# Scattering less from partitions 48-51 in seven groups, and issuing the first eight loads in halves

## The chip, the cores and the metric

The kernel runs on one core of one Trainium2 chip. The metric is the device time of one execution in microseconds (us). Each kernel was timed in several runs, beside runs of the kernel before on the same chip. A ratio is the mean time of one kernel's runs over the mean of the other's of the same rounds, which is not quite the ratio of the medians that I quote beside it. With every ratio comes a 95% interval.

## The reference

Each of 8 batches has 2048 rows of 2560 floats (10 KB a row) and 2048 scores. A row goes to the place that its score has in the sorted order of its batch.

```python
B, N, D = 8, 2048, 2560
order = np.argsort(scores, axis=1)
ranks = np.argsort(order, axis=1)
out[b_idx, ranks, :] = x
```

There are 168 MB to read and 168 MB to write. The arithmetic is counting, for each score, how many others are smaller.

## The kernel before

VectorE (DVE) counts the ranks, batch after batch. A batch's rows are moved in eight groups of 256 rows, two rows a partition. Most groups go through SBUF, the core's on-chip memory: GpSimd (POOL) issues a **load** of 2.5 MB into one of eight buffers, and later two indirect **scatters** of 128 rows each.

```python
GROUPS = [(256 * i, 2) for i in range(8)]
DIRECT = range(6)
...
BULK = [(b, g) for b in range(B) for g in range(len(GROUPS)) if g or b not in DIRECT]
NBUF = 8
LAG = 4
...
for k, (b, g) in enumerate(BULK):
    i = k % NBUF
    if k >= LAG and k + NBUF - LAG < len(BULK):
        scatters_done(pl, k - LAG)          # waits for all 16 increments of both scatters
        load(pl, k + NBUF - LAG, s_load[(k - LAG) % NBUF])
    ...                                     # wait for load k and for its ranks
    for j in range(GROUPS[g][1]):
        scatter(k, j)                       # 128 rows of 10 KB, indirect
```

The first group of batches 0 to 5 doesn't pass through SBUF. SyncE (SP) and ScalarE (ACT) each read 128 ranks a batch into registers and issue one DMA for each row, from HBM (the chip's main memory) to HBM, in loops of 16 rows. I call these **direct rows**: 768 on SP's queue and 768 on ACT's.

```python
for b in DIRECT:
    for h, (line, name) in enumerate(((sp, ENG.SP), (act, ENG.Activation))):
        ...
        with line.eng.Fori(0, half // G) as q:          # G = 16 rows a turn of the loop
            _, at = nc.values_load_multi_w_load_instructions(...)
            for i in range(G):
                ...
                line.eng.dma_start(
                    out=out_bytes[bass.ds(at[i], ROW)], in_=x_bytes[...],
                ).then_inc(s_rows[line], 16)
```

In the packet records of this kernel a direct row is cut into 16 pieces of 640 bytes (12288 such packets in each row queue, for 768 rows), one for each of the 16 DMA engines. A load or scatter over 128 partitions is 128 packets, of 20 KB (two rows; 7296 for 57 loads) or 10 KB (one row; 14848 for 116 scatters): eight an engine. The records of the engine that is left alone in the tail agree: eight scatter packets between one 4-byte semaphore packet of q0 and the next, and in each row queue a 640-byte packet and a 4-byte one by turns.

Of the kernel before, what the change touches and what calls it, by code (L numbers as in the profile page):

```python
# [7 lines left out]
P = 128  # L8
F32 = mybir.dt.float32
BF16 = mybir.dt.bfloat16  # L10
I32 = mybir.dt.int32
U8 = mybir.dt.uint8
OP = mybir.AluOpType
ENG = mybir.EngineType
# [26 lines left out]
def kernel(  # L41
# [6 lines left out]
    nc = tc.nc  # L48
    B, N, D = x.shape
    C = N // P  # L50
# [11 lines left out]
    LAG = 4  # L62
    G = 16

    STEPS = [(0, 1), (1, 2), (2, 4), (4, 8)]

    def first_col(g):
        return GROUPS[g][0] // P if g < len(GROUPS) else C
# [11 lines left out]
    acc = [pool.tile([P, B * C], F32, name=f"acc{i}") for i in range(3)]  # L80
    rank = pool.tile([P, B * C], F32, name="rank")
    rank_i = pool.tile([P, B * C], I32, name="rank_i")
    rows_i = {b: pool.tile([1, WIDE], I32, name=f"rows_i{b}") for b in DIRECT}
    xb = [pool.tile([P, MMAX * D], F32, name=f"x{i}") for i in range(NBUF)]
    ps_col = psum.tile([P, 512], F32, name="ps_col")
# [7 lines left out]
    with tc.tile_critical(no_gpsimd_drain=True):  # L93
# [12 lines left out]
        s_rows = {sp: nc.alloc_semaphore("rows_sp"), act: nc.alloc_semaphore("rows_act")}  # L106
        n_scat = [[0] * MMAX for _ in range(NBUF)]

        def load(line, k, sem):
            b, g = BULK[k]  # L110
            r, m = GROUPS[g]
            line.eng.dma_start(  # L112
                out=xb[k % NBUF][:, :m * D],
                in_=x[b, r:r + P * m, :].rearrange("(p j) d -> p (j d)", j=m),
            ).then_inc(sem, 16)


        sp.eng.dma_start(out=s_in[:], in_=scores).then_inc(s_scores, 16)
        load(sp, 0, s_first)


        t_zero = pl.did(nc.gpsimd.memset(ident[:], 0.0))  # L122
# [52 lines left out]
        def broadcast(b):  # L175
            pe.after(dve, t_copied)
            ticks = []
            for c in range(C):
                pe.did(
                    nc.tensor.transpose(  # L180
                        out=ps_all[:, P * c:P * (c + 1)],
                        in_=s_col[:, c, b:b + 1].to_broadcast([P, P]),
                        identity=ident[:],
                    )
                )
                if c % 4 == 3:
                    ticks.append(pe.n)
            return ticks
# [3 lines left out]
        dve.after(pl, t_mask)  # L192
        bc = broadcast(0)

        def ranks(b, g_lo, g_hi):

            for g in range(g_lo, g_hi):
                lo = first_col(g)
                m = GROUPS[g][1]
                for j in range(m):  # L200
                    col = b * C + lo + j
                    score = s_col[:, lo + j, b:b + 1]
                    dve.after(dve, dve.n)

                    def count(i, lo_c, hi_c, do, **how):
                        dve.did(
                            do(  # L207
                                out=trash[i][:, :P * (hi_c - lo_c)],
                                in0=s_all[:, P * lo_c:P * hi_c],
                                accum_out=acc[i][:, col:col + 1],  # L210
                                **how,
                            )
                        )

                    count(
                        0, lo, C, nc.vector.tensor_scalar,
                        scalar1=score, scalar2=None, op0=OP.is_lt, op1=OP.add,
                    )
                    if lo:
                        count(  # L220
                            1, 0, lo, nc.vector.tensor_scalar,
                            scalar1=score, scalar2=None, op0=OP.is_le, op1=OP.add,
                        )
                    count(
                        2, lo, lo + m, nc.vector.scalar_tensor_tensor,
                        scalar=score,
                        in1=mask[:, MMAX - j:MMAX - j + m, :].rearrange("p a b -> p (a b)"),
                        op0=OP.is_equal, op1=OP.mult,
                    )
            cols = slice(b * C + first_col(g_lo), b * C + first_col(g_hi))  # L230
            dve.after(dve, dve.n)
            dve.did(
                nc.vector.tensor_tensor(  # L233
                    out=rank[:, cols], in0=acc[0][:, cols], in1=acc[1][:, cols], op=OP.add
                )
            )
            dve.after(dve, dve.n)
            dve.did(
                nc.vector.tensor_tensor(  # L239
                    out=rank[:, cols], in0=rank[:, cols], in1=acc[2][:, cols], op=OP.add  # L240
                )
            )
            dve.after(dve, dve.n)
            tick = dve.did(
                nc.vector.tensor_copy(out=rank_i[:, cols], in_=rank[:, cols])  # L245
            )
            for g in range(g_lo, g_hi):
                t_bulk[b, g] = tick

        def rows_to_psum(b):  # L250
            pe.after(dve, dve.n)
            for j in range(GROUPS[0][1]):
                pe.did(
                    nc.tensor.transpose(  # L254
                        out=ps_row[:1, P * j:P * (j + 1)],
                        in_=rank[:, b * C + j:b * C + j + 1],
                        identity=ident[:],
                    )
                )

        def rows_to_bytes(b):
            dve.after(pe, pe.n)
# [11 lines left out]
        for b in range(B):  # L274
            dve.after(dve, dve.n)
            for q in range(4):
                dve.after(pe, bc[q])
                t_copied = dve.did(
                    nc.vector.tensor_copy(  # L279
                        out=s_all[:, 512 * q:512 * (q + 1)],  # L280
                        in_=ps_all[:, 512 * q:512 * (q + 1)],
                    )
                )
            steps = STEPS if b == 0 else [(0, len(GROUPS))]
            for lo, hi in steps:
                ranks(b, lo, hi)
                if lo == 0:
                    if b in DIRECT:
                        rows_to_psum(b)
                        rows_to_bytes(b)  # L290
                    if b + 1 < B:
                        bc = broadcast(b + 1)


        for b in DIRECT:
            for h, (line, name) in enumerate(((sp, ENG.SP), (act, ENG.Activation))):
                line.after(dve, t_rows[b])
                half = WIDE // 2
                with line.eng.Fori(0, half // G) as q:
                    _, at = nc.values_load_multi_w_load_instructions(  # L300
                        rows_i[b][:, bass.ds(half * h + q * G, G)],
                        engines=[name],
                        min_val=b * N * ROW,
                        max_val=(b * N + N - 1) * ROW,
                        skip_runtime_bounds_check_because=(
                            "a rank counts other scores of one batch of N, so it lies in 0..N-1"
                        ),
                    )
                    for i in range(G):
                        row = b * N + GROUPS[0][0] + half * h + i  # L310
                        line.eng.dma_start(
                            out=out_bytes[bass.ds(at[i], ROW)],
                            in_=x_bytes[bass.ds(q * (G * ROW) + row * ROW, ROW)],
                        ).then_inc(s_rows[line], 16)
        for line in (sp, act):
            line.wait(s_rows[line], 16 * len(DIRECT) * WIDE // 2)


        def scatters_done(line, k):
# [4 lines left out]
        def scatter(k, j):  # L324
            b, g = BULK[k]
            col = b * C + first_col(g) + j
            n_scat[k % NBUF][j] += 1
            nc.gpsimd.indirect_dma_start(  # L328
                out=out_flat,
                out_offset=bass.IndirectOffsetOnAxis(ap=rank_i[:, col:col + 1], axis=0),  # L330
                in_=xb[k % NBUF][:, j * D:(j + 1) * D],
                in_offset=None,
                element_offset=b * N * D,
            ).then_inc(s_scat[k % NBUF][j], 16)

        for k in range(1, NBUF):
            load(pl, k, s_load[k])
        for k, (b, g) in enumerate(BULK):
            i = k % NBUF
            if k >= LAG and k + NBUF - LAG < len(BULK):  # L340
                scatters_done(pl, k - LAG)
                load(pl, k + NBUF - LAG, s_load[(k - LAG) % NBUF])
            if k == 0:
                pl.wait(s_first, 16)
            else:
                pl.wait(s_load[i], 16 * (k // NBUF + (i > 0)))
            pl.after(dve, t_bulk[b, g])
            for j in range(GROUPS[g][1]):
                scatter(k, j)
# [34 lines left out]
```

## Time and profile before

| | before |
|---|---|
| time, median | 792.58 us (4 runs, 791.97 to 792.9) |
| span of the profiled run | 791.4 us |
| DVE, POOL busy | 50%, 18% |
| loads and scatters: packets of POOL's queue q0 | 24912 |
| SP's queue q1, ACT's queue q10 | 24736, 24576 |

The lines that say what bounds it, the DMA share by slices and the windows at the end, are in the prediction below. Here are the page's DMA queues (packets, MB, and the time of those packets as a share of the span of 16 engines):

```profile
q0 software_dynamic: 24912, 301.48, 89.5%
q1 hardware_dynamic: 24736, 10.60, 4.9%
q10 hardware_dynamic: 24576, 7.91, 4.0%
```

The engines spend nine tenths of the span on loads and scatters. And the two row queues, which with the first load move only 18.5 MB, need **as many packets** as these: 24576 = 768 rows x 16 engines x 2, as each piece of a row is followed by a 4-byte packet for its semaphore (on ACT's queue 12288 packets of 640 bytes and 12288 of 4).

### The profile page before, as it was taken

Reading aid. Unit: us, or ns where it says so; the run is one execution under the profiler, and the core shown is the slowest. Engines: PE = TensorE matmul, PEld = TensorE weight load, DVE = VectorE, ACT = ScalarE, POOL = GpSimd, SP = SyncE. Lnnn points to the kernel's source line nnn. Section 1 sums busy time; section 2 is a strip of 40 time slices with the busy share of each in tenths; the row PEclk is TensorE's granted clock in tenths of the full one; section 3 lists DMA queues with packets and bytes.
Section 4 is the critical chain, followed back from the end, with each engine's and each line's share of the span. In section 5 each row is a group of like instructions: output and inputs, shape, how many; then the busy total and the mean of one; then the engine's idle time right before and its main releaser. Section 6 shows DMA issues by size and latency. Waiting matters only on the chain.

```text
span 791.4 us, 7991 instructions
## 1 busy us (share of the span) xinstructions
PE 30.9 (4%) x156; PEld 27.6 (3%) x156; DVE 398.3 (50%) x809; ACT 0.0 (0%) x1; POOL 146.2 (18%) x182
## 2 busy tenths in 40 slices
PE   4000010020100200200000000000000000000000
PEld 3000010010100100200000000000000000000000
DVE  5999999999999999999992000000000000000000
ACT  0000000000000000000000000000000000000000
POOL 2114021212121211112121212121111212121000
PEclk9655555555555555655555555555555555555555
DMA  8999999999999999999999999999999999999960
GB/s 366 423 407 416 425 416 423 418 425 415 427 414 425 415 424 416 425 420 422 419 419 421 420 422 420 422 418 423 418 424 419 422 419 423 418 425 418 417 252 19
DMA packets 74239, 320.12 MB, mean 404 GB/s; under 512 B 27368, under 2 KB 51944, under 8 KB 51944
## 3 DMA queue, kind: packets, MB, share of 16 engines
q0 software_dynamic: 24912, 301.48, 89.5%
q1 hardware_dynamic: 24736, 10.60, 4.9%
q10 hardware_dynamic: 24576, 7.91, 4.0%
q14 instruction: 14, 0.11, 0.0%
q8 instruction: 1, 0.02, 0.0%
HBM read 167.84 MB, written 167.77 MB: 424 GB/s over the span
## 4 chain that ended last, share of the span: by engine, by line
DVE 43%; another core or an unknown queue 30%; POOL 8%; DMA 6%; issue 6%; PE 3%; POOLq 0%; SPq 0%
DVE trash L207 41%; POOL out_dram L328 6%; DMA x<-in_x_dram 6%; PE ps_all L180 2%; POOL x L112 2%; DVE s_all L279 1%; PE ps_row L254 0%; DMA s_in<-in_scores_dram 0%; PE ps_col L159 0%; DVE rank_i L245 0%; DVE rank L239 0%; DVE rank L233 0%; POOLq L350 0%; POOLq L28 0%
## 5 line engine op out<-in xcount | busy, mean ns | idle before, releaser
L207 DVE TENSOR_SCALAR_CACHE_REDUCE trash<-s_all,s_col 128x1792 bf16<-128x1792 f32 (+7 forms) x240 | 315.2, 1348 | 4.6
L328 POOL DMA_INDIRECT out_dram<-x,rank_i x116 | 112.3, 968 | 146.1 <-DVE rank_i L245 55.7
L112 POOL DMA_DIRECT2D x<-in_x_dram x57 | 32.1, 566 | 462.2 <-DMA out_dram<-x,rank_i 441.1
L207 DVE SCALAR_TENSOR_TENSOR trash<-s_all,s_col,mask 128x256 bf16<-128x256 f32 x128 | 61.6, 481 | 0.0
L180 PE MATMUL ps_all<-ident,s_col 128*128 128x128 f32 x128 | 26.5, 394 | 1.2 <-DVE s_all L279 0.8
L180 PEld LDWEIGHTS ps_all<-ident,s_col 128*128 128x128 f32 x128 | 25.1, 214 | 2.0 <-DVE s_all L279 1.1
L279 DVE COPY s_all<-ps_all 128x512 f32<-128x512 f32 x32 | 21.4, 689 | 6.0 <-PE ps_all L180 5.3
L207 DVE DVE_READ_ACCUMULATOR trash<-s_all,s_col 128x1 f32 x240 | 19.9, 83 | 0.0
L254 PE MATMUL ps_row<-ident,rank 128*1 128x128 f32 x12 | 3.5, 396 | 288.9 <-DVE rank_i L245 288.9
L207 DVE DVE_READ_ACCUMULATOR trash<-s_all,s_col,mask 128x1 f32 x128 | 10.7, 83 | 0.0
L254 PEld LDWEIGHTS ps_row<-ident,rank 128*1 128x1 f32 x12 | 0.5, 81 | 291.1 <-DVE rank_i L245 291.1
L264 DVE TENSOR_SCALAR rows_i<-ps_row 1x256 int32<-1x256 f32 x6 | 2.5, 411 | 4.1 <-PE ps_row L254 4.1
L167 DVE COPY s_col<-ps_col 128x128 f32<-128x128 f32 x1 | 0.3, 292 | 5.0 <-PE ps_col L159 5.0
L159 PE MATMUL ps_col<-ident,s_in 8*128 8x8 f32 x16 | 2.1, 264 | 4.1 <-DMA s_in<-in_scores_dram 4.1
L245 DVE CAST rank_i<-rank 128x16 int32<-128x16 f32 (+3 forms) x11 | 2.0, 180 | 0.4
L159 PEld LDWEIGHTS ps_col<-ident,s_in 8*128 8x128 f32 x16 | 2.0, 211 | 4.1 <-DMA s_in<-in_scores_dram 4.1
L239 DVE TENSOR_TENSOR rank<-rank,acc 128x16 f32<-128x16 f32 (+3 forms) x11 | 1.9, 170 | 0.4
L233 DVE TENSOR_TENSOR rank<-acc,acc 128x16 f32<-128x16 f32 (+3 forms) x11 | 1.9, 170 | 0.4
L140 POOL TENSOR_SCALAR_AFFINE_SELECT mask<-mask 128x256 f32<-128x256 f32 x2 | 0.8, 399 | 0.0
L152 DVE MEMSET acc<- 128x128 f32 x1 | 0.2, 165 | 1.1 <-SPq L93 1.1
L123 POOL MEMSET mask<- 128x512 f32 x1 | 0.5, 525 | 0.0
L122 POOL MEMSET ident<- 128x128 f32 x1 | 0.2, 204 | 0.5 <-SPq L93 0.5
(6 smaller groups left out, 0.7 us busy)
## 6 DMA issues: line engine op xcount, KB each, us to landing
x<-in_x_dram POOLq DMA_DIRECT2D x57, 2560.0 KB, 46.3
out_dram<-in_x_dram ACTq DMA_DIRECT2D x768, 10.0 KB
out_dram<-in_x_dram SPq DMA_DIRECT2D x768, 10.0 KB
x<-in_x_dram SPq DMA_DIRECT2D x1, 2560.0 KB, 13.2
out_dram<-x,rank_i POOLq DMA_INDIRECT x116, 51.2
s_in<-in_scores_dram SPq DMA_DIRECT2D x1, 64.0 KB
```

Of the source, the lines that this page charges most:

```text
L112: line.eng.dma_start(out=xb[k % NBUF][:, :m * D], in_=x[b, r:r + P * m, :].rearrange("(p j) d -> p (j d)", j=m),).then_inc(sem, 16)
L140: nc.gpsimd.affine_select(out=part, in_=part, pattern=[[0, MMAX], [-1, P]], compare_op=OP.is_ge, fill=0.0, base=-half, channel_multiplier=1,)
L159: nc.tensor.transpose(out=ps_col[:, B * c:B * (c + 1)], in_=s_in[:, r + j:r + m * P:m], identity=ident[:B, :B],)
L180: nc.tensor.transpose(out=ps_all[:, P * c:P * (c + 1)], in_=s_col[:, c, b:b + 1].to_broadcast([P, P]), identity=ident[:],)
L207: do(out=trash[i][:, :P * (hi_c - lo_c)], in0=s_all[:, P * lo_c:P * hi_c], accum_out=acc[i][:, col:col + 1], **how,)
L233: nc.vector.tensor_tensor(out=rank[:, cols], in0=acc[0][:, cols], in1=acc[1][:, cols], op=OP.add)
L239: nc.vector.tensor_tensor(out=rank[:, cols], in0=rank[:, cols], in1=acc[2][:, cols], op=OP.add)
L245: nc.vector.tensor_copy(out=rank_i[:, cols], in_=rank[:, cols])
L254: nc.tensor.transpose(out=ps_row[:1, P * j:P * (j + 1)], in_=rank[:, b * C + j:b * C + j + 1], identity=ident[:],)
L264: nc.vector.tensor_scalar(out=rows_i[b][:].rearrange("o (p j) -> o p j", p=P), in0=ps_row[:1, :WIDE].rearrange("o (j p) -> o p j", p=P), s ...
L279: nc.vector.tensor_copy(out=s_all[:, 512 * q:512 * (q + 1)], in_=ps_all[:, 512 * q:512 * (q + 1)],)
L328: nc.gpsimd.indirect_dma_start(out=out_flat, out_offset=bass.IndirectOffsetOnAxis(ap=rank_i[:, col:col + 1], axis=0), in_=xb[k % NBUF][:, ...
```

## The change

In seven groups (the fifth group of batches 1 to 7) the scatters leave out the rows of partitions 48-51: the ranks there get 2048 added, which a bounds check skips. These 4 partitions x 2 rows x 7 groups = 56 rows are issued as further direct rows: four groups (32 rows) by SP and three (24) by ACT. And the first eight loads are issued as two halves of one row (10 KB) a partition. I took the intent to be that the one slow DMA engine gets less to do. That these partitions are that engine's was my assumption.

```diff
+    THIN = [(b, 4) for b in range(1, B)]
+    HOLES = range(48, 48 + 4)
+    HALVED = range(8)
...
+            for j in range(m if k in HALVED else 1):
+                part = slice(j * D, (j + 1) * D) if k in HALVED else slice(0, m * D)
+                line.eng.dma_start(
+                    out=xb[k % NBUF][:, part], in_=rows[:, part]
+                ).then_inc(sem, 16)
...
+                if (b, g) in THIN:
...
+                            out=rank_i[:, cols], in0=rank[:, cols],
+                            scalar1=hole[:], scalar2=None, op0=OP.add,
...
+        def thin_rows(n, b, g):
+            line, name = ((sp, ENG.SP), (act, ENG.Activation))[n % 2]
...
+            for i in range(4 * m):
+                row = b * N + r + HOLES[i % 4] * m + i // 4
+                line.eng.dma_start(
+                    out=out_bytes[bass.ds(at[i], ROW)],
+                    in_=x_bytes[bass.ds(row * ROW, ROW)],
+                ).then_inc(s_rows[line], 16)
...
+                **(dict(bounds_check=N - 1, oob_is_err=False) if (b, g) in THIN else {}),
```

More of the change, by code (lines that the diff above doesn't have):

```diff
@@ L82 @@
     rank_i = pool.tile([P, B * C], I32, name="rank_i")
+    hole = pool.tile([P, 1], F32, name="hole")
+    thin_i = {k: pool.tile([1, 4 * MMAX], I32, name=f"thin_i{k[0]}_{k[1]}") for k in THIN}
     rows_i = {b: pool.tile([1, WIDE], I32, name=f"rows_i{b}") for b in DIRECT}
@@ L107 @@
         n_scat = [[0] * MMAX for _ in range(NBUF)]
+        n_load = [0] * NBUF
         def load(line, k, sem):
@@ L111, in load @@
             r, m = GROUPS[g]
-            line.eng.dma_start(
-                out=xb[k % NBUF][:, :m * D],
-                in_=x[b, r:r + P * m, :].rearrange("(p j) d -> p (j d)", j=m),
-            ).then_inc(sem, 16)
+            rows = x[b, r:r + P * m, :].rearrange("(p j) d -> p (j d)", j=m)
+            for j in range(m if k in HALVED else 1):
[3 more added lines that the diff above has]
+                ).then_inc(sem, 16)
+                if k:
+                    n_load[k % NBUF] += 1
         sp.eng.dma_start(out=s_in[:], in_=scores).then_inc(s_scores, 16)
         load(sp, 0, s_first)
+        loaded = {0: (s_first, 16 * (2 if 0 in HALVED else 1))}
         t_zero = pl.did(nc.gpsimd.memset(ident[:], 0.0))
@@ L193 @@
         bc = broadcast(0)
+        dve.did(
+            nc.vector.tensor_reduce(
+                out=hole[:],
+                in_=ident[:, HOLES[0]:HOLES[0] + 4],
+                axis=mybir.AxisListType.X,
+                op=OP.add,
+            )
+        )
+        dve.after(dve, dve.n)
+        dve.did(
+            nc.vector.tensor_scalar(
+                out=hole[:], in0=hole[:], scalar1=float(N), scalar2=None, op0=OP.mult
+            )
+        )
         def ranks(b, g_lo, g_hi):
@@ L248, in ranks, with rows_to_psum @@
                 t_bulk[b, g] = tick
-        def rows_to_psum(b):
+                if (b, g) in THIN:
+                    cols = slice(b * C + first_col(g), b * C + first_col(g + 1))
+                    dve.after(dve, dve.n)
+                    t_bulk[b, g] = dve.did(
+                        nc.vector.tensor_scalar(
+                            out=rank_i[:, cols],
+                            in0=rank[:, cols],
+                            scalar1=hole[:],
+                            scalar2=None,
+                            op0=OP.add,
+                        )
+                    )
+        def rows_to_psum(b, g):
             pe.after(dve, dve.n)
-            for j in range(GROUPS[0][1]):
+            for j in range(GROUPS[g][1]):
+                col = b * C + first_col(g) + j
                 pe.did(
@@ L255, in rows_to_psum @@
                         out=ps_row[:1, P * j:P * (j + 1)],
-                        in_=rank[:, b * C + j:b * C + j + 1],
+                        in_=rank[:, col:col + 1],
                         identity=ident[:],
@@ L259, in rows_to_psum, with thin_to_bytes @@
                 )
+        def thin_to_bytes(b, g):
+            m = GROUPS[g][1]
+            dve.after(pe, pe.n)
+            t_rows[b, g] = dve.did(
+                nc.vector.tensor_scalar(
+                    out=thin_i[b, g][:].rearrange("o (j i) -> o j i", j=m),
+                    in0=ps_row[:1, :P * m].rearrange("o (j p) -> o j p", j=m)[
+                        :, :, HOLES[0]:HOLES[0] + 4
+                    ],
+                    scalar1=float(b * N),
+                    scalar2=float(ROW),
+                    op0=OP.add,
+                    op1=OP.mult,
+                )
+            )
         def rows_to_bytes(b):
@@ L288 @@
                     if b in DIRECT:
-                        rows_to_psum(b)
+                        rows_to_psum(b, 0)
                         rows_to_bytes(b)
@@ L292 @@
                         bc = broadcast(b + 1)
+                for g in range(lo, hi):
+                    if (b, g) in THIN:
+                        rows_to_psum(b, g)
+                        thin_to_bytes(b, g)
+        n_rows = {sp: 0, act: 0}
+        def thin_rows(n, b, g):
+            line, name = ((sp, ENG.SP), (act, ENG.Activation))[n % 2]
+            r, m = GROUPS[g]
+            line.after(dve, t_rows[b, g])
+            _, at = nc.values_load_multi_w_load_instructions(
+                thin_i[b, g][:],
+                engines=[name],
+                min_val=b * N * ROW,
+                max_val=(b * N + N - 1) * ROW,
+                skip_runtime_bounds_check_because=(
+                    "a rank counts other scores of one batch of N, so it lies in 0..N-1"
+                ),
+            )
+            for i in range(4 * m):
[4 more added lines that the diff above has]
+                ).then_inc(s_rows[line], 16)
+                n_rows[line] += 1
+        todo = list(enumerate(THIN))
         for b in DIRECT:
+            while todo and todo[0][1][0] < b:
+                n, where = todo.pop(0)
+                thin_rows(n, *where)
             for h, (line, name) in enumerate(((sp, ENG.SP), (act, ENG.Activation))):
@@ L314 @@
                         ).then_inc(s_rows[line], 16)
+                n_rows[line] += half
+        for n, where in todo:
+            thin_rows(n, *where)
         for line in (sp, act):
-            line.wait(s_rows[line], 16 * len(DIRECT) * WIDE // 2)
+            line.wait(s_rows[line], 16 * n_rows[line])
         def scatters_done(line, k):
@@ L333, in scatter, with load_ahead @@
                 element_offset=b * N * D,
+                **(dict(bounds_check=N - 1, oob_is_err=False) if (b, g) in THIN else {}),
             ).then_inc(s_scat[k % NBUF][j], 16)
+        def load_ahead(k):
+            i = k % NBUF
+            load(pl, k, s_load[i])
+            loaded[k] = (s_load[i], 16 * n_load[i])
         for k in range(1, NBUF):
-            load(pl, k, s_load[k])
+            load_ahead(k)
         for k, (b, g) in enumerate(BULK):
-            i = k % NBUF
             if k >= LAG and k + NBUF - LAG < len(BULK):
                 scatters_done(pl, k - LAG)
-                load(pl, k + NBUF - LAG, s_load[(k - LAG) % NBUF])
-            if k == 0:
-                pl.wait(s_first, 16)
-            else:
-                pl.wait(s_load[i], 16 * (k // NBUF + (i > 0)))
+                load_ahead(k + NBUF - LAG)
+            pl.wait(*loaded[k])
             pl.after(dve, t_bulk[b, g])
```

## The prediction

Its sum: for the slow engine it is 786.75 - 21.3 + 1.9 + 0.35 = 767.7 us, for the second slowest 767.1 + 2.25 + about 0.4 = 769.7 us, so 17 us less and 775.5 us. The ground for the 21.3 us, that all 56 packets come off one engine, the slow one, and that the skipped indices leave nothing, was my assumption, and no trace had shown it.

> **What bounds the kernel now.** I read the page's shares and slices first, then the waits, then the tail in windows, then the times at which each DMA raised its semaphore. No compute engine is the bound: DVE is 50% busy, POOL 18%, and both are done long before the end. The DMA engines are full.
>
> ```profile
> PE 30.9 (4%) x156; PEld 27.6 (3%) x156; DVE 398.3 (50%) x809; ACT 0.0 (0%) x1; POOL 146.2 (18%) x182
> ...
> DVE  5999999999999999999992000000000000000000
> ...
> DMA  8999999999999999999999999999999999999960
> GB/s 366 423 407 416 425 416 423 418 425 415 427 414 425 415 424 416 425 420 422 419 419 421 420 422 420 422 418 423 418 424 419 422 419 423 418 425 418 417 252 19
> ```
>
> The third row is the one that counts: 420 GB/s in nearly every slice, until the last two. POOL's largest wait, 441 us for earlier scatters to free a buffer, is only this back-pressure. The windows over the end (stretch and length in us, busy time of five engines, clock, DMA share, GB/s) show what happens there:
>
> ```profile
> 740.00:755.00 15.00, 0.00 (x0) 0.00 (x0) 0.00 (x0) 0.00 (x0) 3.35 (x4) 0.50 1.03 416
> 755.00:765.00 10.00, 0.00 (x0) 0.00 (x0) 0.00 (x0) 0.00 (x0) 0.39 (x1) 0.50 0.89 348
> 765.00:770.00 5.00, 0.00 (x0) 0.00 (x0) 0.00 (x0) 0.00 (x0) 0.00 (x0) 0.50 0.09 35
> 770.00:786.50 16.50, 0.00 (x0) 0.00 (x0) 0.00 (x0) 0.00 (x0) 0.00 (x0) 0.50 0.06 26
> ```
>
> From 770 to 786.5 us the share is 0.06, which is one engine of 16 (0.0625), at 26 GB/s, about a sixteenth of the 416 of before. So **one DMA engine finishes some 20 us after the other fifteen**, and the kernel ends with it. It isn't one odd transfer. The last scatter's 16 semaphore increments come at 763.3 us (the first), +1.6 (the fourteenth), +4.1 (the fifteenth) and +23.8 (the last). That last increment was 2.8 us behind the first at 88 us, 6.4 at 192, 10.3 at 297, 13.8 at 402, 17.9 at 507, 20.8 at 612 and 23.4 at 716: one engine loses about 3.4 us in every 105 us. In the records of single packets, 10 KB scatter packets take 385 ns, but 575 of them take some 15 to 60 ns more, and these hardly ever overlap one another, as if they belonged to one engine.
>
> [...] Packet records carry no engine, so the trace can't confirm which one lags. [...] 16 increments spread over 23.8 us. [...] in the tail the lone engine alternates one scatter packet (10 KB), one packet of SP's row queue and one of ACT's.
>
> **The change part by part.** The costs are from the packet records of the tail, where one engine can be followed alone (start to next start): 381 ns for a 10 KB packet, 28 ns for the 640 B an engine moves of an HBM-to-HBM row, 6 ns for a semaphore packet. So one row costs every engine 28 + 6 = 34 ns. A 20 KB load packet takes 757 ns.
>
> Removed: seven groups x two scatters x four rows = 56 rows. [...] 56 x 381 ns = **21.3 us**. This nearly equals the lag of 23.8 us, and the groups are spread evenly (one a batch), so the lag should be knocked back by about 3 us in each batch from 1 on.
>
> Added on every engine: the same 56 rows HBM to HBM, 56 x 34 ns = **1.9 us**. The full engines can't hide it.
>
> Halving eight loads: 64 more packets an engine, each pair 2 x 381 - 757 = 5 ns dearer, 0.3 us, and eight semaphore packets, 0.05 us: **0.35 us**. What I think it is for: with one packet from each queue per turn, the rows are carried as fast as the loads and scatters have packets. From 20 us, when the rows begin, an engine has about 1541 load, scatter and semaphore packets and 1536 packets (768 rows, data and semaphore) in each row queue, an even match. The change lengthens SP's queue to 800 rows (1600 packets) and ACT's to 792; the halves that are still to come at 20 us give some 47 more turns. So row queues and scatters should still end together.
>
> Other added work: seven times on DVE a masked add and a small conversion with a wait on PE (about 0.2 + 0.4 + 0.7 us from like rows), 9 us over a DVE that idles half the span. Batch 1's ranks are there at 110.8 us and its first scatter lands at 143 us, so a microsecond or two is hidden. POOL's seven more load issues of 0.56 us come before its first scatter at 25.6 us. Hidden too.
>
> Sum, by when an engine ends (semaphore times):
> - the slow one: 786.75 - 21.3 + 1.9 + 0.35 = 767.7 us (766.3 if the 56 were slow packets at 25 ns more)
> - the second slowest (767.1 to 767.4, behind by 14 instruction-fetch packets of 0.31 us, I guess): 767.1 + 2.25 + about 0.4 for more code = 769.7 us
> - the other fourteen: 764.9 + 2.25 = 767.1 us.
>
> The end moves from 786.75 to about 769.7 us: 17 us less. Time 792.55 - 17 = **775.5 us**, a ratio of 0.978. Once the slow engine is level, the second slowest is the bound.
>
> **The rivals.**
> 1. **The holes are not on the slow engine**, or skipped indices lead to the remaining 124 rows being dealt out anew over 16 engines. Then the tail stays, each engine gets the 2.25 us (less up to 1.3 us if the saving is shared), and the time is 793 to 795 us. Against: 21.3 us fits the lag too well to be chance. For: nothing in the trace names the engine, and no scatter here has a bounds check.
> 2. **Row queues become the end.** The slow engine loses 56 turns, so at its last scatter it still has some 30 to 40 rows in each row queue. Run at 34 ns this is 2 to 3 us and is in the sum already; if rows without scatters run slower, or SP is held back by the full queue (its last row was issued at 759.6 us, with waits of 2.5 us and more for space), the end comes 2 to 5 us later: 777 to 780 us, and "same".
> 3. **More than hoped.** If the second slowest engine isn't touched by more code or the fetches fall on another engine, all end at 767 us and the time is 773 us.
> 4. **The tail was hidden anyway.** Against it: the span runs to 791.4 us with nothing but this engine at work after 770 us.
>
> **Range and chances.** I give the mechanism 85%; inside it the gain is 17 us give or take 2.5, and 2% is 15.9 us, so about two cases in three of these are over 2%. Predicted 775.5 us, range 770.5 to 782. Faster by over 2%: 0.57; within 2%: 0.41; slower: 0.02.
>
> **What would show each step.** In windows of the changed kernel the stretch with a DMA share of 0.06 is gone or under 4 us. The gap between the first and last of 16 increments swings between 2 and 7 us all along and doesn't grow to 24. GB/s in the middle slices stays at 420. The row queues have 1792 more packets in all for data (56 x 16) and as many semaphores. POOL still waits hundreds of us for scatters, and DVE ends near 410 us. I am wrong if the lone engine remains (rival 1), if row packets alone fill the last microseconds (rival 2), or if the halved loads run at a lower rate than 420 GB/s before 60 us.

## The result, and the profile after

The changed kernel takes **782.06 us** (4 runs, 781.49 to 782.53) against 792.58: 10.5 us less. The ratio is 0.9868, interval 0.9851 to 0.9885, so within 2%. I had said 775.5 us and a range up to 782.0. The sign and the cause of the gain were right, the gain is 0.62 of what I had worked out.

The changed kernel's slices (DMA share in tenths, GB/s) and its queues:

```profile
DMA  8999999999999999999999999999999999999995
GB/s 360 418 419 419 426 415 425 415 421 416 424 418 424 416 421 417 425 417 423 419 421 420 422 419 421 420 422 422 417 425 416 426 416 425 417 424 418 419 415 101
...
q0 software_dynamic: 25920, 300.90, 90.7%
q1 hardware_dynamic: 25904, 10.93, 5.5%
q10 hardware_dynamic: 25344, 8.16, 4.5%
```

The middle is as before at 420 GB/s. Before, the last two slices read 252 and 19 GB/s; now they read 415 and 101: the long tail is gone. But the windows over the end of the changed kernel (same columns as in the prediction) show another one:

```profile
755.00:760.00 5.00, 0.00 (x0) 0.00 (x0) 0.00 (x0) 0.00 (x0) 0.00 (x0) 0.50 1.02 412
760.00:765.00 5.00, 0.00 (x0) 0.00 (x0) 0.00 (x0) 0.00 (x0) 0.00 (x0) 0.50 1.04 321
765.00:770.00 5.00, 0.00 (x0) 0.00 (x0) 0.00 (x0) 0.00 (x0) 0.00 (x0) 0.50 0.99 86
770.00:775.00 5.00, 0.00 (x0) 0.00 (x0) 0.00 (x0) 0.00 (x0) 0.00 (x0) 0.50 0.18 9
```

From 765 to 770 us **all sixteen engines are busy (0.99) and move only 86 GB/s**. This is no lone engine, which would read 0.06. The share counts the time of packets, not their bytes, so these are packets that take long and carry little. The DMA view of the changed kernel from 763.5 us to the end names them:

```profile
q1 hardware_dynamic: 875, 0.28, 13.1%
q10 hardware_dynamic: 490, 0.15, 10.8%
q0 software_dynamic: 36, 0.29, 2.5%
```

875 + 490 packets of direct rows against 36 of scatters. In the same stretch of the kernel before there were 90 + 88. The records of single packets give the order of events: the last 10 KB scatter packet ends at 769.30 us (786.68 before), the last direct row at 773.29 us on ACT's queue and at **775.36 us on SP's**; the span ends 4.4 us later. So the scatters end near where I had expected (769.7 us), and 6.06 us of direct rows come after them. The question for the experiments is why the rows were late, and whether anything else hides in the difference.

### The profile page after: what moved, and what is told of

It is laid out like the page before. It is cut to its first block, busy times and chain, and to the rows that moved or that the text cites. A ratio compares the mean times of both kernels' runs of the same rounds, so it can differ in the third digit from the quotient of the medians.

```text
span 779.7 us, 8177 instructions
## 1 busy us (share of the span) xinstructions
PE 35.4 (5%) x170; PEld 30.5 (4%) x170; DVE 399.8 (51%) x825; ACT 0.0 (0%) x1; POOL 150.2 (19%) x189
## 4 chain that ended last, share of the span: by engine, by line
DMA 49%; another core or an unknown queue 19%; DVE 13%; POOL 7%; issue 6%; PE 1%; POOLq 0%; SPq 0%
DMA out_dram<-x,rank_i 43%; DVE trash L238 12%; DMA x<-in_x_dram 6%; POOL out_dram L422 5%; POOL x L126 1%; PE ps_all L196 0%; DVE s_all L339 0%; DMA s_in<-in_scores_dram 0%; PE ps_col L175 0%; POOLq L446 0%; DVE rank_i L276 0%; DVE rank L270 0%; DVE rank L264 0%; PE ps_row L298 0%
## 5 line engine op out<-in xcount | busy, mean ns | idle before, releaser
L126 POOL DMA_DIRECT2D x<-in_x_dram x64 | 35.7, 560 | 445.7 <-DMA out_dram<-x,rank_i 426.6
L238 DVE SCALAR_TENSOR_TENSOR trash<-s_all,s_col,mask 128x256 bf16<-128x256 f32 x128 | 61.6, 481 | 0.0
L196 PE MATMUL ps_all<-ident,s_col 128*128 128x128 f32 x128 | 28.5, 416 | 3.1 <-DVE s_all L339 2.8
L196 PEld LDWEIGHTS ps_all<-ident,s_col 128*128 128x128 f32 x128 | 26.8, 226 | 4.2 <-DVE s_all L339 3.2
L298 PE MATMUL ps_row<-ident,rank 128*1 128x128 f32 x26 | 7.0, 366 | 392.5 <-DVE rank_i L284 335.2
L238 DVE DVE_READ_ACCUMULATOR trash<-s_all,s_col 128x1 f32 x240 | 19.9, 83 | 0.0
L284 DVE TENSOR_SCALAR rank_i<-rank,hole 128x2 int32<-128x2 f32 x7 | 1.6, 228 | 0.2
```

The lines of the kernel that those rows point to most:

```text
L126: line.eng.dma_start(out=xb[k % NBUF][:, part], in_=rows[:, part]).then_inc(sem, 16)
L196: nc.tensor.transpose(out=ps_all[:, P * c:P * (c + 1)], in_=s_col[:, c, b:b + 1].to_broadcast([P, P]), identity=ident[:],)
L238: do(out=trash[i][:, :P * (hi_c - lo_c)], in0=s_all[:, P * lo_c:P * hi_c], accum_out=acc[i][:, col:col + 1], **how,)
L284: nc.vector.tensor_scalar(out=rank_i[:, cols], in0=rank[:, cols], scalar1=hole[:], scalar2=None, op0=OP.add,)
L298: nc.tensor.transpose(out=ps_row[:1, P * j:P * (j + 1)], in_=rank[:, col:col + 1], identity=ident[:],)
```

## The experiments

My theory, called A, is that the engines go on as the lone engine does in the tail of the kernel before: its 129 packets from 770 to 786.5 us are 43 of SP's row queue, 43 of ACT's and 43 of q0, strictly in turn. A direct row (two packets) would then be carried once per two packets of q0. The early halves gave turns at a time when no rows were waiting, so they were wasted, and rows were left over at the end, where they run slowly without company. First the count that supports it. Per engine, from the packet records: how many packets q0 had in a stretch (turns), and how many rows SP's queue moved in it:

| stretch, us | before: turns | half of them | SP rows | after: turns | half of them | SP rows |
|---|---|---|---|---|---|---|
| 20 to 60 | 62.9 | 31.5 | 28.4 | 108.8 | 54.4 | **41.8** |
| 60 to 80 | 53.4 | 26.7 | 26.7 | 54.6 | 27.3 | **19.9** |
| 80 to 400 | 655.6 | 327.8 | 327.6 | 656.8 | 328.4 | 324.2 |
| 400 to 763.5 | 764.8 | 382.4 | 382.6 | 766.9 | 383.5 | 387.0 |
| after 763.5 | 5.2 | | 2.7 | 2.2 | | **27.2** |

Before, rows are half the turns to within 0.2 of a row from 60 us on: there were always rows waiting. In the changed kernel the turns are as many as I had counted (1589 from 20 us on, 1588 predicted), but in the first 60 us some 20 pairs of turns passed without a row. The reason is the issue. The two lines below are the DMA issues of direct rows by SP from 20 to 80 us, first of the kernel before, then of the changed one (count, then shortest, median and longest duration in ns, first and last start):

```profile
L311 SPq DMA_DIRECT2D out_dram<-in_x_dram x67: 520/521/696, 19.9 to 79.3; - x67
```

```profile
L402 SPq DMA_DIRECT2D out_dram<-in_x_dram x64: 3/521/788, 19.4 to 77.6; - x64
```

Before, SP issued 67 rows by 80 us and the engines moved 55 of them, so there was a stock. With the halves the engines moved 61.6 of the 64 issued: the stock was gone, and there was nothing left to carry. SP starts a row every 0.74 us at the median, with a longer gap at each loop turn of 16 rows (2.4 to 3.7 us in this stretch), so (15 x 0.74 + 2.4) / 16 = 0.84 us a row gives it about 1.2 rows a us at most, whatever the turns. The halves were to give 23.5 rows and gave 61.6 - 55.1 = 6.5 (on ACT 64.0 - 55.4 = 8.6).

### The halves taken away, and the holes taken away

```diff
-    HALVED = range(8)
+    HALVED = range(0)
```

> The holes and the thin rows stay, all loads are whole. Theory A (row queues ran short of turns; a row left over at the end costs about 0.4 us of its queue's time): early in the kernel the halves won only 6.5 rows on SP's queue (61.6 against 55.1 done an engine at 80 us), so without them SP is left with about 35 rows instead of 29 at the end of the scatters: 2.6 us longer than the changed kernel, about 784.7 us. Rival B (the halved loads themselves cost the missing time, as shorter packets at the start): 776 to 781 us.

Measured: 784.48 us (783.82 to 784.82, and one run of 790.51), ratio to before 0.9925, interval 0.9884 to 0.9965 (wide because of that one run). The last row on SP's queue ends at 777.66 us, 2.3 us later than in the changed kernel, the last scatter packet at 769.04, about as there. Theory A holds and B falls: the halves don't cost the time. By the medians they win 2.4 us, but the intervals of the two ratios overlap because of that one run.

```diff
-    THIN = [(b, 4) for b in range(1, B)]
+    THIN = []
```

> All scatters whole and no thin rows, only the first eight loads halved. Theory A: the lone engine's tail of some 20 us is back and 64 more packets add 0.35 us: about 792.9 us, the same as before. Rival B (halves take away part of the tail, since rows get more turns): 787 to 790 us.

Measured: 792.57 us, ratio 1.0004, interval 0.9987 to 1.0021. The tail of the lone engine is back; in the windows of this run:

```profile
770.00:775.00 5.00, 0.00 (x0) 0.00 (x0) 0.00 (x0) 0.00 (x0) 0.00 (x0) 0.50 0.06 26
775.00:780.00 5.00, 0.00 (x0) 0.00 (x0) 0.00 (x0) 0.00 (x0) 0.00 (x0) 0.50 0.07 26
```

So the halves alone give nothing. The holes alone give 8.0 us (the run before this one), both together 10.5.

### Eight other loads halved

```diff
-    HALVED = range(8)
+    HALVED = range(16, 24)
```

> The changed kernel with loads 16 to 23 halved instead of 0 to 7, at a time when the row queues are full (some 30 rows waiting an engine). Theory A: eight loads give 9 more turns each, 72 turns or 36 rows a queue, all of them used; minus the 6.5 rows that the early halves had won, SP's 29 left-over rows are gone, and the kernel ends with its last scatter, as at 769.3 us in the changed kernel's trace: about 776 us. Rival C (SP can't issue its rows sooner, whatever the turns): 782 us, unchanged.

Measured: **777.42 us** (777.08, 777.12, 777.72 and one run of 780.58), ratio 0.9823, interval 0.98 to 0.9846, so whether it is over 2% is unclear. The same number of halves, later, takes off 4.6 us. The last scatter packet ends at 769.97 us, and ACT's rows at 766.9, before it. SP's rows end at 770.99, because eight halved loads in a row again outran SP's issue: its rows waiting fell to 3 an engine at 220 us, and 20 were left at 764.75 us. Both theories had a part here: turns decide (A), but only those that SP's issue can follow (C).

### The added rows left out

```diff
             r, m = GROUPS[g]
+            if n >= 0:
+                return
             line.after(dve, t_rows[b, g])
```

> The changed kernel without its 56 thin rows, which are thus never written (a wrong result on purpose). Theory A: both row queues hold 768 rows again and are done with the scatters; the end is the last scatter's, less the 1.9 us that 56 rows cost an engine: 774 to 775 us. Rival D (the skipped indices or the bounds check cost the missing time): 781 to 782 us.

Measured: 775.03 us (774.91 to 775.16), ratio 0.978, interval 0.9763 to 0.9796; the output is wrong. The last scatter packet ends at 768.39 us and the rows before it, at 767.24. The holes, the masked ranks and the bounds check are all still in this kernel, so none of them costs the missing time: rival D falls. It is the 56 rows alone, as issued.

### All added rows on SP

```diff
-            line, name = ((sp, ENG.SP), (act, ENG.Activation))[n % 2]
+            line, name = (sp, ENG.SP)
```

> The changed kernel with all 56 thin rows on SP's queue (824 rows) and none on ACT's (768). In the changed kernel 29 rows of SP's and 17 of ACT's were left at the end of the scatters and took 12 us. If each queue drains by itself at about 0.4 us a row, SP's 53 take 21 us: about 791 us. If the two queues share one rate (46 rows in 12 us, 0.27 us a row), the sum of the rows counts and nothing changes: about 782 us.

Measured: 789.21 us (789.08 to 789.33 and one of 792.11), ratio 0.9971, interval 0.995 to 0.9992. SP's rows end at 785.78 us, ACT's at 763.2. The time is near the first answer, but not for its reason. At 766 us SP had issued 798 of its 824 rows, and 790 of them had been moved; the 26 others follow at 0.74 us each (19 us), the pace of SP's issue. Up to then SP had stood before what looks like a full queue: from 500 us on about 30 rows were always waiting, and the number didn't grow (in the changed kernel 32 at 400, 500 and 600 us). The rows that were in the queue went much faster than 0.4 us: 26.1 an engine from 763 to 767 us, 0.15 us each. In the changed kernel both queues together moved 43.9 an engine from 763 to 770 us, 0.16 us each. So one rate shared by both queues is not ruled out by this run, and fits it. Rows left over cost in two ways: those in the queue about 0.16 us each while nearly all engines are at it, those that found no place in it 0.74 us each.

### Other partitions

```diff
-    HOLES = range(48, 48 + 4)
+    HOLES = range(32, 32 + 4)
```

> The changed kernel with the holes at partitions 32-35, [...] instead of 48-51. Theory A (the holes help because they are on the one slow engine): the lone engine's tail is back, 786.75 + 2.25 us for the last landing, a DMA share of 0.06 at the end, 794 to 795 us. Rival (124 rows instead of 128 help wherever they are): 782 us. [...]

Measured: 800.14 us (799.63 to 800.82), ratio 1.0101, interval 1.0084 to 1.0118. The lone slow engine is back: its last scatter packet ends at 787.57 us. I had expected 794 to 795 us for the whole; the rows that are left over, which I had not reckoned with, end 6 us after the scatters, at 793.5. In a late scatter the first increment (734.9 us) now comes 17 us before the fourteenth: one engine, which I take to be that of partitions 32-35, runs ahead. It wasn't the second slowest, whose gap of 3.6 us behind the fourteenth is still there.

The next run takes partitions 16-19, which I supposed to be the same engine's as 48-51; nothing had shown it before this run.

```diff
-    HOLES = range(48, 48 + 4)
+    HOLES = range(16, 16 + 4)
```

> The changed kernel with the holes at partitions 16-19, [...]. If the engine counts: 782 us, as the changed kernel, no lone engine at the end. If it is the partitions 48-51 themselves that are slow: a lone engine's tail of some length and 785 to 795 us.

Measured: 782.79 us (782.0 to 783.33), ratio 0.9876, interval 0.9859 to 0.9892, as the changed kernel. The last scatter packet ends at 769.23 us; SP's last row comes at 778.78, 3.4 us later than in the changed kernel, as SP issued it only at 777.04. Partitions 16-19 do as well as 48-51, and 32-35 do not: so it isn't the partitions 48-51 themselves that are slow. The three times (782.06, 782.79 and 800.14 us) fit one slow engine that serves both 48-51 and 16-19, but not 32-35.

### Halves spread over the later loads

```diff
-    HALVED = range(8)
+    HALVED = range(31, 58, 3)
```

> The changed kernel with nine loads halved that are spread over the later part (31, 34, ... 55), where the row queues are full and each load alone gives 9 turns, which the issue of rows can follow. Halves on eight loads in a row (16 to 23) had emptied SP's queue (3 rows waiting at 220 us) and left 20 of its rows over. Theory A: 81 turns are 40 rows a queue, all used, none left over at the end: about 776 us, 1 us under the run with loads 16 to 23. Rival (SP's issue is the limit): 777 us and more, with rows left over.

Measured: 778.19 us (778.12 to 778.37), ratio 0.9821, interval 0.9805 to 0.9838. No row is left over: SP's end at 765.09 us, ACT's at 759.41, and the windows of this run at the end are those of scatters alone:

```profile
760.00:765.00 5.00, 0.00 (x0) 0.00 (x0) 0.00 (x0) 0.00 (x0) 0.00 (x0) 0.50 0.99 420
765.00:770.00 5.00, 0.00 (x0) 0.00 (x0) 0.00 (x0) 0.00 (x0) 0.00 (x0) 0.50 0.21 88
770.00:775.00 5.00, 0.00 (x0) 0.00 (x0) 0.00 (x0) 0.00 (x0) 0.00 (x0) 0.50 0.02 8
```

The turns are used as theory A says, but the time isn't 1 us under that of the run with loads 16 to 23; by the medians it is 0.8 us over it, and by the ratios (0.9821 and 0.9823) the two can't be told apart. The last scatter packet ends at 771.20 us instead of 769.97, as all rows now run beside scatters. So leaving the last rows over for the time in which only the slowest engines are at work was no loss here.

### Fewer holes

```diff
-    THIN = [(b, 4) for b in range(1, B)]
+    THIN = [(b, 4) for b in range(1, B, 2)]
...
-    HALVED = range(8)
+    HALVED = range(31, 58, 3)
```

> The run with spread halves, with holes in four groups (batches 1, 3, 5, 7) instead of seven. No rows are left over there, so this measures the removed scatter packets alone: the slow engine has 24 packets of 381 ns more and 24 rows of 34 ns less, 8.3 us: 778.2 + 8.3 = 786.5 us, with a lone engine at the end again. If a hole were worth less than a packet, the time would be nearer 780 us.

Measured: 785.29 us (783.7 to 785.79), ratio 0.9898, interval 0.9881 to 0.9914. The last scatter packet ends at 778.86 us, 7.66 us after that of the run with seven groups, for 8.3 predicted. The lone engine stands alone from 770 us (share 0.06, then 0.05), and the rows had all ended by 761.6. So for these three groups the 381 ns a removed scatter packet fit within a tenth. For the four groups that stay they fit less well: from 786.68 us (before) to 778.86 is 7.8 us, where 32 x (381 - 34) ns, less some 0.4 us for nine halved loads, would be 10.7. These are single profiled runs, and the four runs here spread over 2.1 us; why the first holes bring less stays open.

### Two engines at once

Both of these also have nine groups at 48-51 and ten late halves. The question is whether the partitions that get holes besides, 60-63 in the first and 124-127 in the second, are the second slowest engine's; I chose them without a trace that shows it. The edit of the first, cut; the second has 124 in place of 60.

```diff
-    THIN = [(b, 4) for b in range(1, B)]
-    HOLES = range(48, 48 + 4)
-    HALVED = range(8)
+    THIN = {(b, 4): 48 for b in range(1, B)}
+    THIN |= {(2, 6): 48, (5, 6): 48, (3, 6): 60, (6, 6): 60}
...
+    HALVED = range(30, 58, 3)
```

> Ten late halved loads; holes at 48-51 in nine groups instead of seven, and in two more groups at 60-63, [...]. In the run with spread halves the last scatter ended at 771.2 us on the slowest engine, 769.9 on the second slowest, 767 on the others. [...] both come level and the end is near 768.5 us: about 775.5 us. If it isn't, the second slowest stays the bound and 32 more rows cost each engine 1.1 us: about 778 us.

> The same with 124-127, [...] in place of 60-63. [...] about 775.5 us. If not: about 778 us.

Measured: 778.91 and 778.94 us, ratios 0.9822 (0.9806 to 0.9839) and 0.9828 (0.9811 to 0.9844). Both fall on the "if not" side: by this neither 60-63 nor 124-127 are the second slowest engine's, and more holes for the slowest one gained nothing here while another was just as late (last scatter packets at 772.12 and 771.70 us). The increments of the last scatter agree: with 60-63, one engine is ahead at 762.8 us (the next comes at 766.3) and two are still late, at 770.7 and 772.5 (the fourteenth at 768.9). Which engine the second is, stays open.

## Why the prediction was right or wrong

**Right: the bound, and roughly the size of what comes off, with some luck.** A lone engine set the end, holes at 48-51 or at 16-19 took it off (782.06 and 782.79), and nothing else did (no holes: 792.57; holes at 32-35: 800.14). In the last scatter the gap between the first and the last increment is 6.7 us instead of 23.8. The last scatter packet moved from 786.68 to 769.30 us, 17.4 us, where I had 17. That this is so near is partly luck: 42 rows an engine had not been carried yet, which at my 34 ns would have been another 1.4 us. Where no row was left over (spread halves) the scatters ended at 771.20 us, 15.5 us earlier than before, and the four groups alone brought 7.8 us of 10.7. So the term "56 x 381 ns" was somewhat too large. My sum also mixes two sorts of times: 786.75 us is the end of a packet and the others are semaphore times, by which the slow engine ended at 787.1; this changes nothing at its end, which another engine sets. (And the row of my first lines that shows 420 GB/s is the fourth, not the third.)

**Right: the compute work is hidden.** With the rows left out, all the added work of DVE, PE and POOL is still there, and the time is 775.03 us.

**Wrong: the step "the halves that are still to come at 20 us give some 47 more turns. So row queues and scatters should still end together."** The turns came (1589 for 1588), the rows did not: SP issues at most about 1.2 rows a us, by 80 us it had issued 64, and no number of turns could have moved more. Of 23.5 rows expected from the halves SP's queue got 6.5. I had read the pace of the issue as a wait for room in a full queue (the waits "of 2.5 us and more" of my second rival). The gaps of 2.4 us and more come at the loop's turns, once in 16 rows, and are there when the queue is nearly empty as well. Had I set the rows issued by 80 us (67) beside the rows moved (55), both readable before the change, I would have found that only a dozen could be moved earlier.

**Wrong: the price of the rows left over.** I took 34 ns a row, which holds beside scatters, where a 640-byte packet takes 32 ns. Row after row without scatters they are far slower: from 763 to 770 us, with nearly all engines at work, the changed kernel moved 26.6 + 17.3 rows an engine, 0.16 us each, nearly five times the price. A 640-byte packet of SP's took 150 to 165 ns on average from 767 to 770 us, one of ACT's 190 to 270 ns from 764 to 767 us. Together these two make the 6.06 us between the last scatter packet and the last row. My second rival named this end ("if rows without scatters run slower, or SP is held back by the full queue ... 777 to 780 us") but stopped 2 us short. It had allowed for 30 to 40 rows in each row queue; what it had wrong was their price.

**Wrong in a detail, without cost:** the 56 packets of 10 KB are gone from POOL's queue (16584 = (116 scatters + 14 halves) x 128 - 56), but the skipped indices do leave packets. POOL's queue has 56 more 4-byte packets than its DMAs' semaphores account for (2936 = 64 loads x 16 + 116 scatters x 16 + 56), one for each skipped row; with four groups of holes it is 32 more, with eleven 88. If these lie on the slow engine, as I took the rows that they replace to do, it lost no turns, as I had feared it would; a packet's record doesn't name its engine.

**Open:** why that one engine's 10 KB scatter packets are slower. The trace shows that 523 packets of the changed kernel between 60 and 760 us take over 15 ns more than the usual 385 ns and that they hardly overlap; it doesn't show why. Nor is it shown what makes the rows slow at the end. The lack of scatters alone doesn't: in the run with all added rows on SP, from 776 to 785 us, when rows came one by one as SP issued them, a 640-byte packet took 29 ns at the median (50 ns on average). Which engine is the second slowest, and why the first holes bring less than the last, is open too.

Four of the versions above with a right result are faster than both kernels. The lowest medians are those of the changed kernel with loads 16 to 23 halved, 777.42 us, and with spread halves, 778.19, which is steadier over four runs. Which of the two is faster isn't shown.

## What to carry to other kernels

When the DMA engines are full, look at when each of a DMA's 16 increments comes and not only at the mean share: here one engine that fell 3.4 us behind in every 105 us was paid for once, at the end (23.8 us), and only holes at what I take to be that engine's partitions helped (782.06 and 782.79 us; with holes at 32-35 800.14). When several queues share the engines, count packets as well as bytes: here short packets in one queue were carried in step with the packets of the others (327.6 rows, of two packets each, for 655.6 packets an engine from 80 to 400 us), so what is to run beside the long transfers should be issued while these still last (0.16 us a row left over, 34 ns beside scatters). And before adding room for more issues, check that the issuing engine has a stock waiting there to fill it: by 80 us SP had issued 64 rows and 61.6 of them had been moved.
